# FFN blocks turned by transposing transfers of 16-bit halves instead of by TensorE

## The chip, the cores and the metric

The kernel runs on one core of a Trainium2 chip. Time is device microseconds of one execution of the whole program; the median of three runs is given. The engines are TensorE (PE), VectorE (DVE), ScalarE (ACT), GpSimd (POOL) and SyncE (SP); SP only issues transfers here, and POOL mostly. Each engine takes its instructions in order, and waits where one of them waits.

## The reference, cut to what matters

One layer of a streaming encoder on 512 tokens of width 1024, in float32:

```
x = x + 0.5 * swiglu(rms_norm(x, ffn1_norm), ffn1_w1, ffn1_w3, ffn1_w2)
h = rms_norm(x, mix_norm); p = h @ w_in               # RWKV-7, attention and gate columns
x = x + (gate_a * y_a + gate_b * y_b) @ w_out         # y_a from RWKV-7, y_b from attention
x = x + 0.5 * swiglu(rms_norm(x, ffn2_norm), ffn2_w1, ffn2_w3, ffn2_w2)
out = rms_norm(x, final_norm)

def swiglu(h, w1, w3, w2):
    return (silu(h @ w1) * (h @ w3)) @ w2             # w1, w3: 1024 x 2816, w2: 2816 x 1024
```

The change touches the two FFNs alone.

## The kernel before, in words

The products of float32 matrices are made of three TensorE matmuls each (`mm3`): both operands are split into a high part in a format that the array takes and the low rest; high by high, high by low, low by high. ACT casts the high part, DVE subtracts for the low one.

The hidden units of an FFN are 22 groups of 128. Two of them are computed one by one at the start; the other 20 are five blocks (0 to 4) of 512 units, class `Wide`. A block multiplies with the two-by-two scheme that needs seven products in place of eight: the tokens are two halves of 256, the contraction two halves of 512, and `w1` and `w3` give the other factors. Product n of block b is called the step (b, n), n from 0 to 6. One step is 24 matmuls of 128x512: two halves h of the weights, two halves i of the tokens' rows, two k, three of `mm3`. The weights of a step are sums of parts of `w1` and `w3` that transfers add up: plain loads on SP's queue (`plain`), adding ones on POOL's (`add`). `weight(m + 2, h)` splits the weights of the step after next in the middle of step m (h = 0) and at its end (h = 1), into a ring of four places; it also starts the next transfer into the buffer that it read.

The order of the steps is a list, `s.order`, m counting through it. Blocks 0 and 1 run interleaved at the start; from block 2 on the pattern repeats: (b, 0), two steps that finish block b-1, then (b, 1), (b, 2), (b, 6), (b, 5). What DVE, ACT and PE do stands in the program in the order in which they run (`written(True)`); the places of SP's and POOL's transfers among each other come from the scheduler.

Sums of the products stand in PSUM: X, Y and others, two banks each. `finish(m)` reads them after a step. After (b, 4) DVE adds into `u2` (the tile `u[0]`) and multiplies with `p`, after (b, 3) ACT takes the silu into `sa`, and DVE multiplies `u3` (`u[1]`) with it. `u[0]` and `u[1]` then hold the block's hidden values with tokens on the partitions: `u[half]` is 128 x 2 x 512, two groups i of 128 tokens. The second matrix, `w2` (class `Seven`), wants hidden units on the partitions, so each of the block's four groups f of 128 units is turned: `turn_all` makes 16 TensorE transposes of 128x128 a block into the banks Y (freed by then), and ACT copies four banks into their places in the tiles `rl` and `rh` (`hidden`). They run in the steps (b+1, 1) and (b+1, 2), in two sets of eight with an ACT copy pair each; for block 0 both sets run in (1, 2). Block 4, the last, is turned by `turn` in another place.

The tiles that the step of the change uses: `u` (`u_384`, `u_385` in FFN1), `p` (four tiles, two a block), `sa` (two), `rl`, `rh`. A transposing transfer is in the kernel before already: `tokens` (line 1083) splits a tile of 32-bit values into its low and high 16-bit halves by ACT (line 1086), turns them by a transposing transfer of SP (line 1087), and joins the halves on POOL (line 1089). It runs eight times, ahead of and at the start of FFN2.

Of the kernel before, what the change touches and what calls it, by code (L numbers as in the profile page):

```python
# [12 lines left out]
U16 = mybir.dt.uint16  # L13
# [6 lines left out]
P = 128  # L20
# [62 lines left out]
def kernel(  # L83
# [6 lines left out]
    nc = tc.nc  # L90
# [17 lines left out]
    dve, act, pe = [Queued(e, False) for e in (nc.vector, nc.scalar, nc.tensor)]  # L108
# [22 lines left out]
    ident = cp.tile([P, P], F32, name="ident")  # L131
# [368 lines left out]
    KH, TH, LO, HI = KF // 2, T // 2, slice(0, D // 2), slice(D // 2, D)  # L500

    BLOCKS, EARLY = (KF - 2) // 4, 2
# [147 lines left out]
    class Wide:  # L650


        def __init__(s, hp, kind, nrm, w1, w3, w2, quads, residual, C=None):
            def four(name):
                return [hp.tile([P, 2, T], F32, name=f"{name}{h}")[:] for h in range(2)]

            s.nrm, s.w, s.x, s.residual, s.later = nrm, (w1, w3), quads, residual, ()
            s.seven = sv = kind(hp, w2)
            s.A, s.B, s.C = [four("ca"), four("cd")], four("cb"), C or four("cc")
            s.extra = hp.tile([P, 2, T], F32R, name="extra")  # L660
            s.u = [hp.tile([P, 2, T], F32, name=f"u{i}")[:] for i in range(2)]
            q = [hp.tile([P, 2, 4, TH], F32R, name=f"q{i}") for i in range(3)]
            s.q = {n: (t[:, 0], t[:, 1]) for n, t in zip((1, 4, 3), q)}
            s.small = [hp.tile([P, NB], F32, name=f"sm{n}") for n in range(5)]
            s.end = BLOCKS - 1
            s.order = [(b, n) for n in (0, 6) for b in range(EARLY)]
            s.order += [(0, 1), (0, 2), (0, 4), (0, 5), (1, 1), (0, 3), (1, 2), (1, 4), (1, 5)]
            for b in range(EARLY, BLOCKS):
                s.order += [(b, 0), (b - 1, 3), (b - 1, 4)][:3 if b > EARLY else 2] + [(b, n) for n in (1, 2, 6, 5)]
            s.order += [(s.end, 4), (s.end, 3)]  # L670
            sv.parts = kind.PARTED
            e, o = [t[:].rearrange("p a t -> p (a t)").rearrange("p (b d) -> p b d", b=2) for t in quads]
            flat = [t.rearrange("p a t -> p (a t)") for t in (*s.C, *s.u)]
            sv.wide, sv.fg = s, flat[2]
            sv.O = [o[:, 0], o[:, 1], flat[0], flat[1]]
            sv.e = [t.rearrange("p (k t) -> p k t", t=TH) for t in (e[:, 0], e[:, 1], flat[3][:, 0:3 * TH])]
            a1, a0 = s.chain(s.end - 1), s.chain(s.end)
            sv.sum = [*a1, *s.B, a0[0], a0[1][:, 0:1]]
# [111 lines left out]
                cols = slice(half * TH, (half + 1) * TH)  # L790
                act.copy(s.seven.hidden(2 + 4 * s.end + f)[:, cols], s.turns[f][:, cols])

        def turn_all(s, b, fs):
            for f in fs:
                ps = s.Y[b % 2][f % 2]
                for i in range(4):
                    pe.transpose(ps[:, i * P:(i + 1) * P], s.u[i // 2][:, i % 2, f * P:(f + 1) * P], ident[:])
            for f in fs:
                act.copy(s.seven.hidden(2 + 4 * b + f), s.Y[b % 2][f % 2][:])

        def finish(s, m):
            b, n = s.order[m]
# [95 lines left out]
        def blocks(s, pa, pb, more):  # L898
            sv, end, nrm = s.seven, s.end, s.nrm
            raw = [[t[k][:, 0:TH] for k in range(KD)] for t in (nrm.hi, nrm.lo)]  # L900
            soon = {(0, 0): ((s.sums, 1),), (0, 6): ((s.low, 1),), (1, 6): ((s.low, 2),), (0, 1): ((s.low, 4),),
                    (0, 2): ((s.low, 5),), (0, 5): ((s.low, 3),)}
            todo = {(0, 0): ((s.gated, 0),),
                    (1, 0): ((s.cast, 1), (s.sums, 2)),
                    (0, 6): ((s.cast, 2), (s.sums, 4), (s.back, 0)),
                    (1, 6): ((s.cast, 4), (s.sums, 5), (s.hidden, 1, pa[:], pb[:])),
                    (0, 1): ((s.cast, 5), (s.gated, 1)),
                    (0, 2): ((s.cast, 3),),
                    (0, 5): ((s.cast, 0),),
                    (0, 3): ((s.low, 0), (s.cast, 6)),  # L910
                    (1, 2): ((s.low, 6), *[(s.plain, sv.O[i], s.residual[i]) for i in range(2)]),
                    (2, 5): ((sv.second, 0),), (3, 2): ((sv.two, 0),),
                    (end, 0): ((sv.operand, 0, 0),), (end, 2): ((sv.operand, 0, 1),), (end, 6): ((sv.one, 0),),
                    (end, 5): ((sv.second, 1), (sv.one, 1)), (end, 4): ((sv.two, 1),)}
            for at, steps in more.items():
                todo[at] = tuple(todo.get(at, ())) + steps
            for m, (b, n) in enumerate(s.order):
                apart = n == 4 and (b < EARLY or b == end)
                early = m < 2 * EARLY
                ps = s.X[b % 2] if n in (0, 2, 3, 5) or early else s.X[(b + 1) % 2] if n == 6 or apart else s.Y[b % 2]  # L920
                onto = n in (2, 3, 5) or (n == 6 and early) or (n == 4 and not apart)
                last = m + 2 >= len(s.order)
                if last:
                    sv.slots += s.ring[2 * m % 4:2 * m % 4 + 2]
                for h in range(2):
                    wh, wl = s.ring[(2 * m + h) % 4]
                    for i in range(2):
                        for k in range(2):
                            c = slice(i * P, (i + 1) * P)
                            if early:  # L930
                                qh, ql = [t[4 * (n > 0) + 2 * h + k][:, c] for t in raw]
                            else:
                                qh, ql = [t[:, 2 * h + k, c] for t in s.q[n]]
                            mm3(ps[i][:], qh, ql, wh[:, k], wl[:, k], not onto and h + k == 0, h + k == 2, onto)
                    if b > 1 and (n, h) == (2, 0):
                        s.turn_all(b - 1, (2, 3))
                    if (b, n) == (1, 2):
                        s.turn_all(0, ((0, 1), (2, 3))[h])
                    if h == 1:
                        if m == len(s.order) - 1:  # L940
                            s.turns = dict(zip((0, 2, 1, 3), s.Y[end % 2] + s.X[1 - end % 2]))
                            act.activation(s.sa[0], ps[0][:], AF.Silu)
                            act.activation(s.sa[1], ps[1][:], AF.Silu)
                            s.turn((0, 2), 0)
                            for i in range(2):
                                dve.tensor_tensor(s.u[1][:, i], s.u[1][:, i], s.sa[i], op=ALU.mult)
                            sv.operand(0, 2)
                        else:
                            s.finish(m)
                        if b > 1 and n == 1:  # L950
                            s.turn_all(b - 1, (0, 1))
                    if h == 1:
                        for f, *a in soon.get((b, n), ()):
                            f(*a)
                    if not last:
                        s.weight(m + 2, h)
                    elif len(sv.slots) == 2:
                        sv.weight(0, h)
                    elif h == 0:
                        sv.slots.insert(2, s.last)  # L960
                        sv.weight(0, 2)
                        sv.weight(0, 3)
                    else:
                        sv.weight(0, 4)
                s.gate(m)
                for f, *a in todo.get((b, n), ()):
                    f(*a)
            sv.slots.append(tuple(tmp("g5", (P, 1, T), F32R)[:] for _ in range(2)))
            sv.junk = [tmp(f"osq{i}")[:] for i in range(2)]
            sv.weight(0, 5)  # L970
            sv.run()
# [121 lines left out]
    with ExitStack() as mx:  # L1093
# [102 lines left out]
        for o, c0, mu in ((spare[2], DA, 4), (spare[3], 0, 0)):  # L1196
            ps = bank("pk", pf)
# [3 lines left out]
        for p in range(NP):  # L1201
            za.append((zslots[2 * p], zslots[2 * p + 1]))
            for i, (w_, x_, par0, o) in enumerate(((uw, lw, PAR_W0, zslots[2 * p]), (ux, lx, PAR_A0, zslots[2 * p + 1]))):
                ps = bank("pz", (pr, pf)[i])
# [181 lines left out]
        for t in range(C - 1):  # L1386
            n, m = t + 1, C - 1 - t
# [103 lines left out]
        at = b1.go(range(2))  # L1491
# [9 lines left out]
        at = b1.go(range(2, 5), a0.sum(at))  # L1501
# [3 lines left out]
        at = b1.go(range(5, 7), b0.sum(at))  # L1505
# [16 lines left out]
        at = ahead.go(range(7))  # L1522
# [254 lines left out]
        sees, turned, exps, copies, yb = [], ([], []), [], [], []  # L1777
# [176 lines left out]
        ycs, sqs, pgs, pus, parts = [None] * NP, [None] * NP, [None] * NP, [None] * NP, {}  # L1954
# [70 lines left out]
        ps = proj(0, fox_proj, ybs, fws[0])  # L2025
        for m in range(KD):
# [11 lines left out]
            if m + 1 < KD:  # L2038
                ps = proj(m + 1, fox_proj, ybs, fws[m + 1])
# [29 lines left out]
        for m in range(KD):  # L2069
            g = slot[m]  # L2070
            ps = proj(m, rwkv_proj, ya)
# [136 lines left out]
```

## Time and profile before

| | |
|---|---|
| median of 3 runs | 1082.62 us (1082.43 to 1082.85) |
| profiled execution | 1083.12 us, span 1081.3 us |
| busy: PE / DVE / ACT / POOL | 1072.1 / 829.7 / 677.4 / 223.9 us |
| granted TensorE clock | 0.999 |
| FFN1, steps of the blocks | from 33.3 us on |
| FFN2, first transposing load of its input | 712.4 us |
| bytes moved | 179.23 MB, mean 166 GB/s |

A row of a group or of the sequence reads: line, engine, operation, what is written <- what is read, shapes, how many; then busy time or start and length. `[0.30 <-PE P]` behind a row says how long the engine stood idle ahead of it and what ended that. Line 103 is that of the recording helper through which DVE, ACT and PE instructions pass, so many groups carry it. `SPq` and `POOLq` rows are transfers being issued; their time there is that of the issuing engine, not of the transfer.

### The profile page before, as it was taken

The numbers are of one execution on the slowest core, as the hardware profiler recorded it, in microseconds if no ns is written. First come the engines' busy times: TensorE is split into PE (matmuls) and PEld (weight loads), VectorE is DVE, ScalarE is ACT, GpSimd is POOL, SyncE is SP. The second block draws the span as 40 slices with busy tenths as digits, with TensorE's granted clock in tenths as the row PEclk, the third lists the DMA queues.
The fourth block names the chain that finished last, engine by engine and source line by source line (L and its number), as shares of the span: only waits on it lengthen the run. The fifth ranks groups of instructions, "written<-read, shape, count | busy, mean of one in ns | idle before, by whom it ended". The sixth has DMA issues, their size and how long they took to land.

```text
span 1081.3 us, 16859 instructions
## 1 busy us (share of the span) xinstructions
PE 1072.1 (99%) x6346; PEld 881.2 (81%) x6346; DVE 829.7 (77%) x1155; ACT 677.4 (63%) x1063; POOL 223.9 (21%) x275
## 2 busy tenths in 40 slices
PE   9999999999999999999999999999999999999997
PEld 7888888888887887888878887888888888888886
DVE  7998575789865698888777777866697666699874
ACT  6775556576555666445888876545576555576554
POOL 1221120134202302412000120125321212114210
PEclk9999999999999999999999999999999999999999
DMA  7989978769955443444312244677977979869972
GB/s 209 261 174 229 217 164 207 180 150 187 233 138 167 110 115 95 128 136 118 89 46 81 91 133 148 192 161 205 290 156 178 211 197 188 194 147 203 235 189 78
DMA packets 150543, 179.23 MB, mean 166 GB/s; under 512 B 20542, under 2 KB 86654, under 8 KB 150462
## 3 DMA queue, kind: packets, MB, share of 16 engines
q0 software_dynamic: 33392, 70.14, 33.8%
q1 hardware_dynamic: 116334, 106.58, 33.1%
q10 hardware_dynamic: 736, 1.45, 0.3%
q8 instruction: 50, 0.82, 0.3%
q14 instruction: 31, 0.25, 0.1%
HBM read 163.51 MB, written 12.52 MB: 163 GB/s over the span
## 4 chain that ended last, share of the span: by engine, by line
PE 96%; DVE 2%; ACT 1%; issue 1%; DMA 0%; ACTq 0%; DVEq 0%
PE P L103 40%; PE P L176 6%; PE P L175 6%; PE P L177 6%; PE pgt L103 5%; PE l L103 3%; PE spot L103 3%; PE pq L103 3%; PE ppj L103 2%; PE pk L177 2%; PE pk L175 2%; PE pk L176 2%; PE pw L176 1%; PE pw L177 1%; PE pw L175 1%; PE f L103 1%
## 5 line engine op out<-in xcount | busy, mean ns | idle before, releaser
L103 PE MATMUL P<-sraw,q 128*128 128x512 f32 x344 | 91.3, 389 | 0.0
L103 PEld LDWEIGHTS P<-sraw,q 128*128 128x128 f32 x344 | 64.6, 188 | 13.4
L103 PE MATMUL P<-swhi,q 128*128 128x512 f32 x224 | 71.4, 390 | 0.0
L103 PE MATMUL P<-sraw,wxh 128*128 128x512 f32 x200 | 68.4, 394 | 0.0
L167 ACT CAST whi<-raw 128x1024 fp32r<-128x1024 f32 (+2 forms) x42 | 40.4, 961 | 43.3 <-issue 14.2
L103 PE MATMUL P<-swhi,wxh 128*128 128x512 f32 x144 | 56.9, 395 | 0.0
L103 PE MATMUL P<-swhi,wxl 128*128 128x512 f32 x144 | 56.1, 390 | 0.0
L103 PE MATMUL P<-swlo,wxh 128*128 128x512 f32 x144 | 56.1, 389 | 0.0
L168 DVE TENSOR_TENSOR wlo<-raw,whi 128x1024 fp32r<-128x1024 f32 (+2 forms) x43 | 48.5, 1127 | 9.4 <-ACT whi L167 8.3
L693 POOL DMA_DIRECT2D cd<-in_ffn_w_dram x24 | 29.5, 1229 | 119.2 <-DVE swlo L103 38.3
L693 POOL DMA_DIRECT2D cb<-in_ffn_w_dram x20 | 24.1, 1207 | 144.7 <-DVE cd L103 80.0
L103 PE MATMUL P<-sraw,wxl 128*128 128x512 f32 x136 | 53.0, 390 | 0.0
L103 PEld LDWEIGHTS P<-swhi,q 128*128 128x128 f32 x224 | 42.1, 188 | 8.7
L103 PE MATMUL P<-swlo,q 128*128 128x512 f32 x112 | 43.6, 389 | 0.0
L103 ACT CAST sraw<-cd 128x1024 fp32r<-128x1024 f32 x30 | 31.5, 1050 | 19.0 <-PE P L103 11.5
L103 ACT COPY RD<-spot 32x128 f32<-32x128 f32 (+2 forms) x128 | 39.9, 311 | 5.3 <-PE spot L103 2.3
L103 PEld LDWEIGHTS P<-sraw,wxh 128*128 128x128 f32 x200 | 37.2, 188 | 7.3
L552 POOL DMA_DIRECT2D ca<-in_ffn_w_dram x16 | 19.3, 1205 | 95.8 <-DVE swlo L103 66.5
L103 DVE TENSOR_TENSOR u<-P,u 128x512 f32<-128x512 f32 x52 | 34.1, 684 | 5.8 <-ACT u L103 5.6
L103 DVE TENSOR_TENSOR swlo<-cc,swhi 128x1024 fp32r<-128x1024 f32 x20 | 24.5, 1225 | 18.2 <-ACT swhi L103 17.9
L177 PE MATMUL pk<-xh,wlo 128*128 128x512 f32 x96 | 37.5, 392 | 1.0 <-DVE wlo L168 1.0
L175 PE MATMUL pk<-xh,whi 128*128 128x512 f32 x96 | 38.0, 396 | 0.4 <-DVE u L1241 0.4
(626 smaller groups left out, 3434.4 us busy)
## 6 DMA issues: line engine op xcount, KB each, us to landing
raw<-in_w_in_dram SPq DMA_DIRECT2D x40, 512.0 KB
cc<-in_ffn_w_dram SPq DMA_DIRECT2D x36, 512.0 KB
cb<-in_ffn_w_dram POOLq DMA_DIRECT2D x36, 512.0 KB, 6.1
cb<-in_ffn_w_dram SPq DMA_DIRECT2D x32, 512.0 KB
cd<-in_ffn_w_dram POOLq DMA_DIRECT2D x32, 512.0 KB, 7.4
ca<-in_ffn_w_dram POOLq DMA_DIRECT2D x32, 512.0 KB, 7.3
ca<-in_ffn_w_dram SPq DMA_DIRECT2D x20, 512.0 KB
cd<-in_ffn_w_dram SPq DMA_DIRECT2D x18, 512.0 KB
```

Of the source, the lines that this page charges most:

```text
L103: q.last = do(*a, **kw)
L167: (hi_eng or act).copy(hi[:], raw[:])
L168: (eng or dve).tensor_tensor(lo[:], raw[:], hi[:].bitcast(F32), op=ALU.subtract)
L175: pe.matmul(ps, whi, xhi, start=first, stop=False, skip_group_check=onto)
L176: pe.matmul(ps, whi, xlo, start=False, stop=False, skip_group_check=onto)
L177: return pe.matmul(ps, wlo, xhi, start=False, stop=last, skip_group_check=onto)
L552: nc.gpsimd.dma_start(s.sum[g], src, accum_op=ALU.add)
L693: nc.gpsimd.dma_start(to, s.block(b, n, h), accum_op=ALU.add)
```

## The change

For blocks 0 to 3 of both FFNs the 16 TensorE transposes and four ACT copies of `turn_all` are gone. In their place, at the end of the step that finishes a half (n = 4 finishes `u[0]`, half 0; n = 3 finishes `u[1]`, half 1), `apart` copies each 128 x 512 group of `u[half]` by ACT into 16-bit halves, low ones first, then high ones, 1024 of them; it puts them into `p[b]` (half 0) or `sa` (half 1), which are free then. SP turns each by one transposing transfer of eight 128x128 tiles back into `u[half]`. Three steps later, after the weight split in the middle of the step, `joined` interleaves the halves again by four ACT copies into the places in `rl` and `rh`. Block 4 is turned as before. For blocks 2 and 3 the two finishing steps swap: (b, 4) comes ahead of (b, 3).

```
-                s.order += [(b, 0), (b - 1, 3), (b - 1, 4)][:3 if b > EARLY else 2] + [(b, n) for n in (1, 2, 6, 5)]
+                s.order += [(b, 0)] + [(b - 1, 4)] * (b > EARLY) + [(b - 1, 3)] + [(b, n) for n in (1, 2, 6, 5)]
...
-        def turn_all(s, b, fs):
-            for f in fs:
-                ps = s.Y[b % 2][f % 2]
-                for i in range(4):
-                    pe.transpose(ps[:, i * P:(i + 1) * P], s.u[i // 2][:, i % 2, f * P:(f + 1) * P], ident[:])
-            for f in fs:
-                act.copy(s.seven.hidden(2 + 4 * b + f), s.Y[b % 2][f % 2][:])
+        def apart(s, b, half):
+            for i in range(2):
+                parts = (s.sa if half else s.p[b])[i].bitcast(U16)
+                act.copy(parts.rearrange("p (s c) -> p s c", s=2), s.u[half][:, i].bitcast(U16).rearrange("p (c s) -> p s c", s=2))
+                nc.sync.dma_start(s.u[half][:, i].bitcast(U16).rearrange("p (a t) -> p a t", t=P), parts, transpose=True)
+
+        def joined(s, b, half):
+            turned = s.u[half].rearrange("p i t -> p (i t)").bitcast(U16).rearrange("p (i s f t) -> p f i t s", i=2, s=2, t=P)
+            for f in range(4):
+                to = s.seven.hidden(2 + 4 * b + f)[:, half * TH:(half + 1) * TH].bitcast(U16)
+                act.copy(to.rearrange("p (i t s) -> p i t s", i=2, s=2), turned[:, f])
...
+            joins = []
...
-                    if b > 1 and (n, h) == (2, 0):
-                        s.turn_all(b - 1, (2, 3))
-                    if (b, n) == (1, 2):
-                        s.turn_all(0, ((0, 1), (2, 3))[h])
...
-                        if b > 1 and n == 1:
-                            s.turn_all(b - 1, (0, 1))
...
+                    for at, half, b_ in joins:
+                        if (m, h) == (at, 0):
+                            s.joined(b_, half)
+                if n in (3, 4) and b < end:
+                    s.apart(b, int(n == 3))
+                    joins.append((m + 3, int(n == 3), b))
```

What this does to the order of instructions is shown at two places of FFN1's block 3, whose finishing steps are (3, 4) and (3, 3). The first place is TensorE where the block was turned, around the steps (4, 1) and (4, 2); `P_501` and `P_502` are the banks Y, `u_384` and `u_385` the tiles `u[0]` and `u[1]`.

```order
 L103 MATMUL P_500<-swlo,q_386 128x512
 L103 MATMUL P_500<-swhi,q_386 128x512
-L103 MATMUL P_501<-ident,u_384 128x128 x2
-L103 MATMUL P_501<-ident,u_385 128x128 x2
-L103 MATMUL P_502<-ident,u_384 128x128 x2
-L103 MATMUL P_502<-ident,u_385 128x128 x2
 L103 MATMUL P_495<-sraw,wxh_507 128x512 x2
 L103 MATMUL P_495<-sraw,wxl_508 128x512
```

The eight transposes between the steps are gone and nothing stands in their place; eight more are gone from the middle of (4, 2).

The same place on ScalarE, from the weight split of step (3, 4)'s end to the joining of half 0 (`swhi`, `sraw` are high parts of weights):

```order
 L103 CAST swhi<-cd_379 128x1024
+L103 CAST swhi<-cd_380 128x1024
+L103 COPY p_503<-u_384 128x1024
+L103 COPY p_504<-u_384 128x1024
+L103 CAST sraw<-cd_379 128x1024
 L103 ACTIVATE sa_455<-P_497 128x512
 L103 ACTIVATE sa_456<-P_498 128x512
-L103 CAST swhi<-cd_380 128x1024
-L103 CAST sraw<-cd_379 128x1024
 L103 CAST sraw<-cd_380 128x1024
+L103 COPY sa_455<-u_385 128x1024
+L103 COPY sa_456<-u_385 128x1024
```

The splitting copies of half 0 now stand ahead of the next weights' cast and of the silus into `sa`, and those of half 1 behind them. The joining copies follow later in the same program:

```order
 L103 CAST sraw<-cb_381 128x1024
+L103 COPY rl_372<-u_384 128x512
+L103 COPY rh_375<-u_384 128x512
+L103 COPY rl_373<-u_384 128x512
+L103 COPY rh_376<-u_384 128x512
 L103 COPY u_384<-P_495 128x512
```

They read the turned tile `u_384` where the old copies read the banks, and stand ahead of the copies that write the next block's values into `u_384`. The second place is SP's queue around the same steps (`cc`, `ca` are weight buffers):

```order
 L555 DMA ca_377<-in_ffn_w_dram 128x2x512
 L555 DMA ca_378<-in_ffn_w_dram 128x2x512
-L690 DMA cc_363<-in_ffn_w_dram 128x2x512
-L690 DMA cc_364<-in_ffn_w_dram 128x2x512
+L797 DMA_TRANSPOSE u_384<-p_503 128x8x128
+L797 DMA_TRANSPOSE u_384<-p_504 128x8x128
+L797 DMA_TRANSPOSE u_385<-sa_455 128x8x128
+L797 DMA_TRANSPOSE u_385<-sa_456 128x8x128
```

Four transposing transfers now stand in SP's queue between the loads of the weights; behind them follow the loads of `cc`.

## The prediction

> **What bounds the kernel now.** I read the page first (busy times, the chain that ended last), then TensorE's waits, then the transposes themselves.
>
> ```profile
> PE 1072.1 (99%) x6346; PEld 881.2 (81%) x6346; DVE 829.7 (77%) x1155; ACT 677.4 (63%) x1063; POOL 223.9 (21%) x275
> PE 96%; DVE 2%; ACT 1%; issue 1%; DMA 0%; ACTq 0%; DVEq 0%
> PE warm L312 <- DVE onesr L137: 1.1, 1, 1.1
> PE pk L177 <- DVE wlo L168: 1.0, 2, 0.7
> PE pk L175 <- DVE u L1241: 0.4, 1, 0.4
> ```
>
> TensorE (PE) is busy 99% of the span and is 96% of the chain. The three last rows are all that it waited for: 2.5 us, and none of it in an FFN. So in the FFNs an instruction taken from PE shortens the kernel by the time that it holds the array, and any other engine costs nothing until it makes PE wait.
>
> **What the removed transposes cost.** First the group, then the sequence around one set of eight.
>
> ```profile
> L103 PE MATMUL P<-ident,u x160: 270/272/277, 90.3 to 975.1; 128*128 128x128 f32 x160
> 90.06 0.39 PE L103 MATMUL P<-sraw,wxl 128*128 128x512 f32 x1
> 90.30 1.03 PE L103 MATMUL P<-ident,u 128*128 128x128 f32 x8
> 91.08 0.48 PE L103 MATMUL P<-sraw,wxh 128*128 128x512 f32 x1
> 91.40 0.39 PE L103 MATMUL P<-extra,wxh 128*128 128x512 f32 x1
> 91.63 0.40 PE L103 MATMUL P<-sraw,wxl 128*128 128x512 f32 x1
> ```
>
> There are 160; the change removes the 16 of each of four blocks in both FFNs, 128 in 16 sets of eight, and keeps 32 (the last blocks). The 272 ns of one are no price, since they overlap. The price is what a set adds to the spacing of starts. Matmuls with nothing between start 0.227 us apart (the two `sa` rows further down are six matmuls and 1.36 us apart). From 90.06 to 91.40 there are two such steps, 0.45 us, but 1.34 us pass: a set costs **0.89 us** (0.78 for the eight, 0.11 for the changes in and out). 16 x 0.89 = **14.2 us** off PE. I take this whole.
>
> **What is added, and what hides it.** One step (24 matmuls) is 24 x 0.227 = 5.44 us; a block has seven. The rows below are from FFN1, where block 3 finishes; a step ends where ACT can begin on its second bank, here 191.2.
>
> ```profile
> 189.84 0.60 ACT L103 ACTIVATE sa<-P 128x512 f32<-128x512 f32 x1 [0.30 <-PE P L103]
> 191.20 0.60 ACT L103 ACTIVATE sa<-P 128x512 f32<-128x512 f32 x1 [0.76 <-PE P L103]
> 191.69 1.04 ACT L103 CAST swhi<-cd 128x1024 fp32r<-128x1024 f32 x1
> 202.52 0.59 ACT L103 COPY rl<-P 128x512 f32<-128x512 f32 x1 [2.07 <-PE P L103]
> 203.00 0.59 ACT L103 COPY rh<-P 128x512 f32<-128x512 f32 x1
> 190.85 1.23 DVE L103 TENSOR_TENSOR cd<-cd,cb 128x1024 f32<-128x1024 f32 x1
> 192.00 1.29 DVE L103 TENSOR_TENSOR u<-u,sa 128x512 f32<-128x512 f32 x2
> 196.73 1.28 DVE L103 TENSOR_TENSOR u<-P,u 128x512 f32<-128x512 f32 x2
> 197.93 1.28 DVE L103 TENSOR_TENSOR u<-u,p 128x512 f32<-128x512 f32 x2
> 160.00:200.00 40.00, 40.00 (x186) 33.32 (x185) 27.62 (x29) 22.99 (x30) 7.26 (x6) 1.00 0.82 185
> 880.00:920.00 40.00, 40.00 (x186) 33.29 (x186) 27.67 (x29) 21.93 (x28) 7.26 (x6) 1.00 0.83 185
> ```
>
> (The last two are 40 us stretches: length, busy PE, PEld, DVE, ACT, POOL, the clock, the DMA share, GB/s.) The trace has the same operations once: FFN2's input is split into 16-bit halves by ACT and turned by transposes on SP's queue, and POOL waits for them.
>
> ```profile
> 732.67 1.13 ACT L1086 COPY G<-xS 128x512 uint16<-128x512 uint16 x2
> 723.69 1.24 SPq L1087 DMA_TRANSPOSE G<-G  x1
> 734.45 1.72 SPq L1087 DMA_TRANSPOSE G<-G  x1
> 757.62 8.51 SPq L1087 DMA_TRANSPOSE rh<-rh  x1
> 766.24 4.48 SPq L1087 DMA_TRANSPOSE rl<-rl  x1
> 729.21 1.44 POOL L1089 COPY G<-G 128x512 uint16<-128x512 uint16 x2 [2.45 <-DMA G<-G]
> 739.03 1.88 POOL L1089 COPY G<-G 128x512 uint16<-128x512 uint16 x2 [2.12 <-DMA G<-G]
> 775.05 2.84 POOL L1089 COPY rl<-rl 128x512 uint16<-128x512 uint16 x2 [0.24 <-DMA rl<-rl]
> ```
>
> *ScalarE.* Per half two splitting copies of 1024 halfwords and four joining ones of 512. Two 512-wide copies with a step of two take 1.13 us here, so 2 x 1.1 + 4 x 0.6 = 4.6 us; a block has two halves, 9.2 us, and loses four copies from PSUM (0.59 each): +6.8 us a block, 54 us in all. ACT is busy 22 to 23 of 40 us there and would be at some 29 of 38. It stays hidden as long as the casts that PE needs are not late.
>
> *The path of one half.* Take 191.2, in the times of before, as the end of step (3,4), which now comes first. DVE is free at 192.0, subtracts the two tiles until 193.2 (the `u` pairs start 1.20 apart) and has the first product some 0.7 later, 193.9. ACT copies until 195.0 and 196.1, and SP issues the two transfers then. The joining copies stand behind ACT's cast in the middle of the third step after: 191.2 + 2.5 x 5.44 = 204.8, plus 0.3 to the cast and 1.05 for it: 206.2. So the second transfer has **10.1 us**, the first 11.2. Alone one took 4.58 us (734.45 to 739.03) to 5.52 (723.69 to 729.21) from issue to POOL's start, of which 1.24 and 1.72 hold SP, so two in a row should have landed 1.7 + 5.5 = 7.2 us after 195.0, at 202.2: 4.0 us early. If they are late, ACT waits, and the weight casts, `u`'s copies and DVE stand behind it. The first that PE needs are the two copies of `u`, which free the bank that step (4,5) adds to at 191.2 + 4 x 5.44 = 213.0; with 1.1 us for them and 2.1 for four joins (starts 0.48 apart) the joins may begin at 209.8. Only a lateness beyond 3.6 us reaches PE. The other half runs 5.2 to 5.4 us later with the same room: issued at 200.3 and 201.3, wanted at 211.6, free until 215.2. Cost taken: **0**; bounds 0 and what the rivals give.
>
> *SP and POOL queues.* SP's loads behind the transposes in its queue (the next block's fourth product) are issued once DVE has freed their buffer, about 203.6 (their cast in the middle of step (4,1), behind ACT's copies), when SP, done with the last transfer at 201.3 + 1.7, is free; the cast of what they bring comes in the middle of the fifth step after 191.2, at 215.7, 12 us later, where loads on POOL's queue land in 6.1 to 7.4 us:
>
> ```profile
> cb<-in_ffn_w_dram POOLq DMA_DIRECT2D x36, 512.0 KB, 6.1
> cd<-in_ffn_w_dram POOLq DMA_DIRECT2D x32, 512.0 KB, 7.4
> ```
>
> *DMA engines.* How much room a transfer takes, by the stretches of the existing ones:
>
> ```profile
> 706.00:712.00 6.00, 6.00 (x28) 4.76 (x27) 4.46 (x7) 3.23 (x5) 0.00 (x0) 1.00 0.51 139
> 717.90:723.00 5.10, 5.10 (x24) 4.21 (x23) 2.63 (x5) 2.61 (x4) 3.43 (x4) 1.00 0.88 206
> 990.00:1010.00 20.00, 20.00 (x90) 16.57 (x89) 20.00 (x21) 11.71 (x13) 10.29 (x9) 1.00 1.10 199
> ```
>
> One transfer and one 256 KB store lift the share from 0.51 to 0.88 of 5.1 us, so a transfer takes at most 1.9 us of all engines; four in a 38.1 us block add 0.20 to 0.82: 1.02. In the third row the share is 1.10 and PE is still busy for all of 20.00 us. Reordering (b,4) before (b,3) leaves one step (5.44 us) instead of two between the subtraction that reads bank Y and the next product added to it; that subtraction ends some 3 us after its step. No cost.
>
> **The sum.** The profiled execution took 1083.12 us (span 1081.3), 0.5 above the median 1082.62. 1083.12 - 14.2 = 1068.9 for such an execution, so 1068.4 against the median. I say **1068.5 us**.
>
> **Rivals.**
>
> *1. Transfers in series, and PE waits (slower).* For it: under the burst of loads that opens FFN2, the pair issued at 757.62 landed at 775.05, 17.4 us, and SP itself was held for 8.5 and 4.5 us. With 8.7 us each in series the first half lands at 195.0 + 17.4 = 212.4, 2.6 us after 209.8, and the second 17.4 later at 229.8, against 215.2 + 2.6: 12.0 more. 14.6 us a block, eight blocks, less 14.2: +103 us, **1185**. It decides from 1.8 us a block on (14.2 / 8): four in series from 195.0 that end after 215.2 + 1.8 = 217.0, that is more than 5.5 us each, which is the longest that one took alone. Against it: those 5.5 hold the latency, which overlaps if SP can issue the next, and a block's stretch has no burst of ten loads. The Trainium skill speaks for this rival: "VectorE: DVE Perf Modes" (The three transpose paths; Rules for kernel authors) gives 1309 ns for a 128x128 16-bit tile by DMA against 390 ns on TensorE and advises TensorE where PSUM will do. Estimate by that figure: eight tiles a transfer, 10.5 us, 41.9 a block, more than the block lasts. The rows (4.58 to 5.52 us for eight) stand nearer to the forecast. 0.11.
>
> *2. A little late everywhere.* With six us each in places, or ACT pushed by its 6.8 us, PE waits 0.5 to 1.5 us a block: 1 x 8 = 8 us, **1076.5**. For it: 4.0 us of margin is little. Against: 3.6 us more before PE feels it. 0.13.
>
> *3. Only the first block pays.* Where FFN1 leaves its early steps, ACT already stands 4.26 us behind DVE:
>
> ```profile
> 74.05 1.19 ACT L103 COPY P<-rh 128x512 f32<-128x512 f32 x2 [4.26 <-DVE u L103]
> 82.12 1.22 DVE L103 TENSOR_TENSOR swlo<-cd,swhi 128x1024 fp32r<-128x1024 f32 x1
> 33.28 214.59 PE P L103 x987
> ```
>
> The two splitting copies (2.1 us) come right behind and hold up the casts. That `swlo` ends at 83.34 and PE wants it in the middle of the tenth step, 33.28 + 9.5 x 5.44 = 85.0; if all of the 2.1 us reached it, it would be late, and the casts after it too. A slip of 1 to 2 us in each FFN costs 3 us: **1071.5**. 0.08.
>
> *4. Nothing gained*: the slots are filled by waits elsewhere, **1082.6**. PE waits for nothing in the FFNs, so little speaks for it. 0.03.
>
> **How the numbers follow.** The forecast has 0.65. The range 1067.0 to 1077.0 holds it with rival 3 and most of 2 (0.65 + 0.08 + 0.09, 0.82); below 1067 there is nothing more to remove. Faster by over 0.2% (2.2 us, about what this kernel's timing tells from nothing): forecast, rival 3 and most of 2, 0.83; within it 0.06 (rival 4 and the bad end of 2); slower 0.11 (rival 1).
>
> **What would show it.** Right: 128 fewer `P<-ident,u`, PE busy about 1058, no wait of PE on `u`, `sraw` or `swhi` in the FFNs, ACT near 732 busy, and the first joining copy of each half ended by PE or nothing, not by a transfer. Wrong: rows in which ACT's joining copies wait for `u<-p` or `u<-sa` for more than 3.6 us and PE then for casts; SP held far over 2 us per transpose; casts that wait for `cc` loads.

## The result, and the profile after

The changed kernel takes **1095.18 us** (median of four executions, 1092.15 to 1098.97) against 1082.53 beside it: ratio **1.0118** (95%: 1.0087 to 1.015). It is slower by 12.7 us; 1068.5 was predicted, with 1067 to 1077 as the range. The profiled execution took 1095.48 us, span 1093.7. An execution over 1.5% above the fastest of its kernel is left out of medians, ranges and ratios; that is one each in two runs below (1088.7 and 1089.7 us).

The page of the kernel after, its busy times and its chain, then the two longest lines of TensorE's waits, both new (engine and line that waited, who ended it: us in total, times, longest):

```profile
PE 1064.5 (97%) x6218; PEld 868.4 (79%) x6218; DVE 832.0 (76%) x1155; ACT 721.9 (66%) x1127; POOL 223.2 (20%) x275
PE 75%; DMA 8%; DVE 7%; issue 5%; ACT 3%; POOL 0%; SPq 0%; DVEq 0%; ACTq 0%; POOLq 0%
PE P L103 <- DVE p L103: 10.2, 2, 5.6
PE P L103 <- DVE u L103: 4.8, 6, 1.9
```

The 128 transposes are gone (6346 to 6218 matmuls), but PE is busy only 7.6 us less instead of 14.2, and it is idle for 1093.7 - 1064.5 = 29.2 us, where it was idle for 1081.3 - 1072.1 = 9.2. Transfers and DVE have taken a part of the chain that was PE's. What ACT waits for, in the same kernel:

```profile
ACT rl L103 <- DMA u<-sa: 19.2, 4, 6.6
ACT swhi L103 <- DMA cc<-in_ffn_w_dram: 18.5, 2, 9.7
ACT swhi L103 <- DMA cd<-in_ffn_w_dram: 6.5, 2, 5.5
```

The joining copies of half 1 (`u<-sa`) waited four times; those of half 0 (`u<-p`) do not appear. The casts of `cc` waited twice, once in each FFN, and that is the wait that reached PE. The sequence of FFN1's last block shows how, engine by engine:

```profile
190.97 1.20 POOL L693 DMA_DIRECT2D cb<-in_ffn_w_dram  x1 [9.09 <-DVE cd L103]
193.57 3.65 SPq L797 DMA_TRANSPOSE u<-p  x2
195.76 1.20 POOL L693 DMA_DIRECT2D cb<-in_ffn_w_dram  x1 [3.59 <-DVE cd L103]
197.00 1.20 POOL L693 DMA_DIRECT2D cd<-in_ffn_w_dram  x1
198.41 8.20 SPq L797 DMA_TRANSPOSE u<-sa  x2
199.34 1.20 POOL L693 DMA_DIRECT2D cd<-in_ffn_w_dram  x1 [1.13 <-DVE extra L103]
206.71 2.12 SPq L690 DMA_DIRECT2D cc<-in_ffn_w_dram  x2
207.70 1.07 ACT L103 CAST q<-rl 128x1024 fp32r<-128x1024 f32 x1
217.54 1.04 ACT L103 CAST swhi<-cc 128x1024 fp32r<-128x1024 f32 x1 [8.77 <-DMA cc<-in_ffn_w_dram]
218.62 1.23 DVE L103 TENSOR_TENSOR swlo<-cc,swhi 128x1024 fp32r<-128x1024 f32 x1 [8.42 <-ACT swhi L103]
219.76 1.28 DVE L103 TENSOR_TENSOR p<-P,p 128x512 f32<-128x512 f32 x2
220.59 0.76 PE L103 MATMUL P<-swhi,q 128*128 128x512 f32 x1 [4.64 <-DVE p L103]
```

Read it from the top. Four adding loads of POOL (`cb`, `cd`) stand around half 1's two transposing transfers, which hold SP for 8.20 us; half 0's, with one adding load ahead of them, hold it for 3.65. The load of `cc` behind them is issued at 206.71 and lands at 217.5, 10.8 us later. ACT has been free since 208.77. DVE's subtraction for these weights waits for ACT's cast, and behind it, in DVE's order, stands the sum into `p` that frees the bank PE needs. PE does not wait for a transpose or for `cc`; it waits for `p`, three instructions down the line.

What the DMA engines did meanwhile, as windows (length, busy PE, PEld, DVE, ACT, POOL, clock, DMA share, GB/s), first the kernel before, then the one after:

```profile
160.00:175.00 15.00, 15.00 (x76) 12.60 (x75) 8.12 (x8) 7.82 (x12) 1.41 (x2) 1.00 0.91 218
```

```profile
160.00:175.00 15.00, 15.00 (x68) 12.41 (x67) 8.00 (x8) 7.50 (x10) 1.20 (x1) 1.00 1.33 122
160.00:200.00 40.00, 39.07 (x171) 31.66 (x170) 26.96 (x28) 28.09 (x37) 6.68 (x6) 1.00 1.13 207
```

Between 160 and 175 us block 2's half 1 is turned (its pair holds SP from 157.71 for 8.62 us): the engines are at a share of 1.33 and move 122 GB/s; before, 0.91 and 218. They are full and move little.

### The profile page after: what moved, and what is told of

It is laid out like the page before. It is cut to its first block, busy times and chain, and to the rows that moved or that the text cites. A ratio compares the mean times of both kernels' runs of the same rounds, so it can differ in the third digit from the quotient of the medians.

```text
span 1093.7 us, 16755 instructions
## 1 busy us (share of the span) xinstructions
PE 1064.5 (97%) x6218; PEld 868.4 (79%) x6218; DVE 832.0 (76%) x1155; ACT 721.9 (66%) x1127; POOL 223.2 (20%) x275
## 2 busy tenths in 40 slices
DMA packets 184336, 187.62 MB, mean 172 GB/s; under 512 B 54334, under 2 KB 120446, under 8 KB 184254
## 3 DMA queue, kind: packets, MB, share of 16 engines
q0 software_dynamic: 33392, 70.14, 35.0%
## 4 chain that ended last, share of the span: by engine, by line
PE 75%; DMA 8%; DVE 7%; issue 5%; ACT 3%; POOL 0%; SPq 0%; DVEq 0%; ACTq 0%; POOLq 0%
PE P L103 22%; PE P L177 5%; PE P L175 5%; PE P L176 5%; PE pgt L103 5%; PE l L103 3%; PE spot L103 3%; DMA u<-sa 3%; PE pq L103 3%; DMA cc<-in_ffn_w_dram 2%; PE ppj L103 2%; PE pk L175 2%; PE pk L177 2%; PE pk L176 2%; PE pw L176 1%
## 5 line engine op out<-in xcount | busy, mean ns | idle before, releaser
L103 PE MATMUL P<-swhi,q 128*128 128x512 f32 x224 | 74.1, 402 | 11.0 <-DVE p L103 10.2
L167 ACT CAST whi<-raw 128x1024 fp32r<-128x1024 f32 (+2 forms) x42 | 40.3, 960 | 43.7 <-issue 14.2
L176 PE MATMUL pk<-xl,whi 128*128 128x512 f32 x96 | 37.5, 391 | 0.0
```

Source lines behind the costliest of these rows:

```text
L103: q.last = do(*a, **kw)
L167: (hi_eng or act).copy(hi[:], raw[:])
L176: pe.matmul(ps, whi, xlo, start=False, stop=False, skip_group_check=onto)
```

## The experiments

The theory after the traces: *the transposing transfers share the DMA engines badly with the adding loads of the same steps; half 1's and the `cc` load behind them are late, and in the last block that reaches PE.* Rivals: the added ACT copies (they are on the way of every cast); SP's queue alone; the bytes, not the turning; lateness that gathers over the blocks.

**The transfers taken out.** The transfer's line is deleted, so the blocks are not turned; the joining copies read the same tile in another pattern.

```
-                nc.sync.dma_start(s.u[half][:, i].bitcast(U16).rearrange("p (a t) -> p a t", t=P), parts, transpose=True)
```

> The changed kernel without its transposing transfers; ScalarE's splitting and joining copies stay, and the joining ones read the tile unturned (so the hidden units of four blocks reach the second matrix unturned: part of the computation is left out). Theory A (the transfers, by being late and by holding SP's queue, cost all that was lost): 1068.5 us, 1067 to 1071, and no wait of TensorE above 1 us in the FFNs. Rival B (ScalarE's extra copies, 45 us by the page of the change, push the casts late): 1080 us or more.

1072.34 us, ratio 0.9906 (0.9892 to 0.9921). All ACT copies, the order and the waits among engines are there, and the time is 23 us below the change. So ACT's added work is hidden, and the loss lies in the transfers.

**The same bytes, not turned.**

```
-                nc.sync.dma_start(s.u[half][:, i].bitcast(U16).rearrange("p (a t) -> p a t", t=P), parts, transpose=True)
+                nc.sync.dma_start(s.u[half][:, i].bitcast(U16), parts)
```

> The changed kernel with each transposing transfer replaced by a plain one of the same 256 KB between the same tiles on the same queue (the values stay unturned). Theory A1 (turning is what makes a transfer slow: 184,336 packets against 150,543, about 1,000 of under 512 B for each): 1069 to 1073 us. Rival A2 (any further 8 MB on SP's queue at these places does it): 1088 us or more.

1072.49 us, ratio 0.9907 (0.9892 to 0.9921): like no transfer at all. The place of half 1's transfers in SP's queue, in this kernel:

```profile
194.60 1.42 SPq L797 DMA_DIRECT2D u<-sa  x2
197.76 2.01 SPq L690 DMA_DIRECT2D cc<-in_ffn_w_dram  x2
```

1.42 us of SP against 8.20, same queue, same 2 x 256 KB. It is the turning that costs, not the bytes nor one more transfer in the queue. A turned transfer also goes in more packets (184,336 in all on the page, against 155,152 here); no run separates that from the turning.

**Block 3 back on TensorE** (blocks 0 to 2 by transfers).

```
-                if n in (3, 4) and b < end:
+                if n in (3, 4) and b < end - 1:
+        # turn_all of before, for b - 1 == 3 alone, in the steps (4, 1) and (4, 2)
```

> Blocks 0 to 2 of each FFN turned by transfers, block 3 by TensorE as before. Theory C (of 13.4 us lost in FFN1 some 11 are lost in the last block, where the load of cc for (4,4) was issued at 206.7, behind the transposes, and landed at 217.5): 12 sets gone are 10.7 us, about 2.4 us of small stalls stay in each FFN, so 1082.5 - 10.7 + 4.8 = 1076.6, 1075 to 1079. Rival D (every block's transfers cost about the same): 1082.5 + 12.6 x 6/8 = 1092.

1077.2 us (1074.8 to 1079.66), ratio **0.9943** (0.9927 to 0.996): faster than before, and within the 1075 to 1079 expected. Three of four blocks by transfers gain 5.2 us where 12 sets are worth 10.7, so 5.5 us are lost there too; the fourth block turned the gain into the loss.

**Block 3 alone by transfers**, the counterpart.

```
-                if n in (3, 4) and b < end:
+                if n in (3, 4) and b == end - 1:
+        # turn_all of before for blocks 0 to 2, in the places of before
```

> Only block 3 is turned by transfers, blocks 0 to 2 by TensorE: the counterpart of the run with blocks 0 to 2. If the loss lies in the last block, where the load of cc for step (4,4) has only two steps, and does not need the transfers of the blocks before: PE waits 4 to 6 us for p once in each FFN and each FFN loses 8 to 11 us there, less two sets of eight transposes (1.8): 1094 to 1102 us. If lateness gathers over the blocks (DMA engines that never catch up): block 4 is hardly late and the kernel takes 1080 to 1086.

1097.76 us (1097.14 to 1097.91), ratio 1.0139 (1.0126 to 1.0152). TensorE's first wait and ACT's first wait for loads of this kernel:

```profile
PE P L103 <- DVE p L103: 8.4, 2, 5.1
ACT swhi L103 <- DMA cc<-in_ffn_w_dram: 16.7, 2, 9.3
```

The net loss is there whole, with nothing turned by transfers in the blocks before: 15.2 us slower although four sets (3.6 us) are gone, so block 3's transfers cost 18.8 us. Lateness that gathers over the blocks falls.

**The `cc` load on another queue.** For the last block it goes to POOL's queue, past SP's transposes.

```
+                if end:
+                    nc.gpsimd.dma_start(here, s.block(b, 4, h))
-                if b != 1:
+                elif b != 1:
                     s.plain(here, s.block(b, 4, h))
```

> The changed kernel with one load moved: the weights of step (4,4), 2 x 512 KB into cc, are issued on GpSimd's queue instead of SP's, where they stood behind the transposes. Theory C1 (SP's queue, held 8.2 us by the second pair, makes that load late): it is issued at about 202 instead of 206.7 and lands by 211, TensorE's wait of 4.6 us and the slow clock behind it go: about 8 us less in each FFN, 1079 us, 1076 to 1084. Rival C2 (the DMA engines are full, share 1.3 there, so the order in the queue does not matter): 1092 to 1098.

1100.3 us (1098.35 to 1103.62), ratio 1.0167 (1.0145 to 1.0189): no better, and above both ranges expected. Its POOL, SP and ACT:

```profile
204.75 0.76 POOL L715 DMA_DIRECT2D cc<-in_ffn_w_dram  x1 [1.30 <-DVE swlo L103]
201.32 12.02 SPq L799 DMA_TRANSPOSE u<-sa  x2
220.54 1.04 ACT L103 CAST swhi<-cc 128x1024 fp32r<-128x1024 f32 x1 [8.90 <-DMA cc<-in_ffn_w_dram]
```

The load is issued as soon as its buffer is free, 204.75, and still lands at 220.5, 15.8 us later. Time saved in the queue is lost at the DMA engines: SP's queue is where the wait stood, not why.

**The transfers by themselves.** A kernel that computes nothing: groups of transfers, each group begun when the last one has landed; a copy by DVE (`seen<-dst`) or ACT (`seen<-wt`) of two elements shows each landing. Its transposing and its adding transfer:

```
nc.sync.dma_start(dst[i][:].rearrange("p (a t) -> p a t", t=P), src[i][:], transpose=True)
nc.gpsimd.dma_start(wt[i][:], weights(i), accum_op=ALU.add)
```

> Transfers by themselves, with no other work: one transpose of 128 x 1024 halfwords, twice; four in a row, twice; four adding loads of 512 KB alone; four transposes with four adding loads, twice; six plain loads of 512 KB alone; four transposes with six plain loads; four plain copies of the same bytes alone; four plain copies with four adding loads. The layer is not computed. Theory T1 (transposes are slow whatever runs beside them, and follow one another in series): one lands 4.5 to 5.5 us after issue, four take 16 us or more also alone, and plain loads or adding loads change that by less than a third. Theory T2 (they are slowed by the adding loads): four alone land within 10 us, 12 us or more beside adding loads, within 11 beside plain loads. Theory T3 (any load slows them): four alone within 10 us, 12 us or more beside either kind. In all three the plain copies of the same bytes land within 8 us alone and 10 beside adding loads.

DVE's sequence, for four transposes alone (begun behind the `src` row), with four adding loads (the second such group), and with six plain loads:

```profile
18.41 0.10 DVE L24 MEMSET src<- 128x1 uint32 x4
21.86 0.17 DVE L24 COPY seen<-dst 128x2 uint16<-128x2 uint16 x1 [3.35 <-DMA dst<-src]
...
25.76 0.17 DVE L24 COPY seen<-dst 128x2 uint16<-128x2 uint16 x1 [1.02 <-DMA dst<-src]
...
71.07 0.36 DVE L24 MEMSET wt<- 128x2 f32 x4
74.21 0.17 DVE L24 COPY seen<-dst 128x2 uint16<-128x2 uint16 x1 [2.77 <-DMA dst<-src]
86.73 0.17 DVE L24 COPY seen<-dst 128x2 uint16<-128x2 uint16 x1 [12.35 <-DMA dst<-src]
94.67 0.17 DVE L24 COPY seen<-dst 128x2 uint16<-128x2 uint16 x1 [7.77 <-DMA dst<-src]
95.56 0.17 DVE L24 COPY seen<-dst 128x2 uint16<-128x2 uint16 x1 [0.73 <-DMA dst<-src]
...
107.06 0.56 DVE L24 MEMSET wt<- 128x2 f32 x6
112.14 0.17 DVE L24 COPY seen<-dst 128x2 uint16<-128x2 uint16 x1 [4.52 <-DMA dst<-src]
...
123.81 0.17 DVE L24 COPY seen<-dst 128x2 uint16<-128x2 uint16 x1 [0.62 <-DMA dst<-src]
```

| group | last transpose, copy or (where alone) load landed after | spacing |
|---|---|---|
| 4 transposes of 256 KB alone | 7.4 us | 1.2 to 1.4 us |
| 4 plain copies of 256 KB alone | 4.5 us | 0.66 us |
| 4 transposes with 4 adding loads of 512 KB | 22.8 and 24.6 us | |
| 4 transposes with 6 plain loads of 512 KB | 16.9 us | |
| 4 plain copies with 4 adding loads | 8.7 us | |
| 4 adding loads alone | 14.1 us | 2.5 us per 512 KB |
| 6 plain loads alone | 10.7 us | 1.35 us per 512 KB |

A transpose alone is quick: 3.4 us to landing, 1.2 to 1.4 us behind another (the four above are 7.4 us together), so T1 falls. Beside four adding loads the second one lands 13 to 16 us after the group began, where a plain copy in its place took 3.3 (129.0 to 132.33); T2's first half holds. Its second half does not: plain loads slow transposes too, 16.9 us, which is T3's number. The plain loads there are 3 MB in a row, though, the adding ones 2 MB. In both mixes the group takes about the sum of its parts: 7.4 + 10.7 = 18.1 us for the plain loads, 7.4 + 14.1 = 21.5 for the adding ones. The kernel itself has to say which loads matter there.

**The adding loads made plain, in the changed kernel.** The sums of the weights are left out; bytes, places and queue are the same.

```
-            nc.gpsimd.dma_start(to, s.block(b, n, h), accum_op=ALU.add)
+            nc.gpsimd.dma_start(to, s.block(b, n, h))
```

> The changed kernel with the adding loads of the FFN blocks replaced by plain loads of the same bytes into the same places on the same queue, so the sums of the weights are left out and the result is another one. T2 (adding loads are what slows the transposes): every half in time, 1071 to 1075 us, no wait of PE for p. T3 or T1 (any traffic, or the transposes themselves): joins of half 1 still wait 4 to 7 us, PE still waits some 5 us for p in each FFN, 1088 to 1096 us.

**1071.54 us** (1071.19 to 1072.08), ratio 0.9898 (0.9884 to 0.9912), with all 32 transposing transfers. Its page, SP's rows and ACT's at the place shown above:

```profile
PE 1058.0 (99%) x6218; PEld 866.6 (81%) x6218; DVE 830.1 (78%) x1155; ACT 724.7 (68%) x1127; POOL 196.0 (18%) x275
188.67 2.62 SPq L797 DMA_TRANSPOSE u<-p  x2
193.52 3.13 SPq L797 DMA_TRANSPOSE u<-sa  x2
196.74 1.73 SPq L690 DMA_DIRECT2D cc<-in_ffn_w_dram  x2
204.76 1.05 ACT L103 CAST swhi<-cc 128x1024 fp32r<-128x1024 f32 x1
```

Half 1 holds SP for 3.13 us, `cc` is issued at once, and neither its cast nor the joins wait. The window from 160 to 175 us, at 1.33 and 122 GB/s in the change, has 0.87 and 235 here. With the run of plain copies this settles which transfers do it: the transposes with plain loads cost little (1071.5 us), the adding loads with plain copies cost little (1072.5), the two together cost over 20 us. What stays open is why: an adding load also holds the engines almost twice as long (2.5 us to 1.35) and goes in more packets (33,392 on POOL's queue against 25,712 here, for the same 70.14 MB), and no run separates that from a conflict of the two kinds.

**The order alone**: the kernel before with only the swap of (b, 3) and (b, 4).

> The kernel before with only the swap of the finishing steps, (b, 4) ahead of (b, 3); the blocks are turned by TensorE. If the swap costs nothing, as the prediction took it: 1082.4 us (1081.8 to 1083). If the shorter distance between the subtraction and the next product in the same bank is felt, or the turns wait for u: 1084 or more. Its middle stage should last the 522.6 us of before; if the swap were what lengthens it, 524.

1082.63 us, ratio 1.0 (0.9991 to 1.0009). The swap costs nothing, as the prediction had it.

**Versions that gain.** First, block 3's second half by TensorE in one set of eight, and half 1 of blocks 1 and 2 joined a step later:

```
+                        if b == end and n == 1:
+                            s.turn_all(b - 1)          # half 1 alone, eight transposes
-                    joins.append((m + 3, int(n == 3), b))
+                    joins.append((m + 3 + int(n == 3 and b > 0), int(n == 3), b))
```

> Block 3's second half is turned by TensorE (8 transposes at the end of step (4,1)); the halves of blocks 0 to 2 and block 3's first half stay with the transfers, and the second halves of blocks 1 and 2 are joined one step later (at the fourth step after, still ahead of the copy that writes the tile again). If only the second halves come late and only block 4's cc load suffers, as the trace of the change says: the 1072.4 us of the run without transfers plus two sets of eight transposes (2 x 0.89), 1074.2 us (1073.5 to 1076), below the kernel before and below the run with three blocks. If the first half of block 3 is enough to delay the cc load: 1078 to 1086.

Median 1077.7 us, but executions from 1071.3 to 1084.4; ratio 0.9952 (0.9931 to 0.9972). The median lies between the two ranges expected. Without the last block's trouble the same lateness comes out elsewhere, as this row of ACT in block 3 shows:

```profile
183.18 1.04 ACT L103 CAST swhi<-cc 128x1024 fp32r<-128x1024 f32 x1 [8.98 <-DMA cc<-in_ffn_w_dram]
```

Then block 3 wholly by TensorE, as above, with the same line for the later join:

> Block 3 wholly turned by TensorE, as in the run with three blocks, and the second halves of blocks 1 and 2 joined one step later. If the lateness of second halves is what kept that run (1077.2 us) from the sum: 1072.4 + 4 sets x 0.89 = 1076.0 us (1075.5 to 1077), with a narrow spread. If ACT's waits at the joins cost nothing there: the same 1077.2 as that run.

Median 1077.9 us, 1072.5 to 1086.3, ratio 0.9958 (0.9933 to 0.9983). Not the 1076.0 expected, and a wider spread than the run with three blocks. A later join alone moves ACT's wait from the join to the next cast, as the row above shows for the run before this one.

Then the transfers themselves moved, with four blocks turned as in the change: half 1 of blocks 1 to 3 is split and transferred one step later, behind the adding loads, and joined one step later.

```
-                if n in (3, 4) and b < end:
+                if b < end and (n == 4 or (b, n) == (0, 3)):
                     s.apart(b, int(n == 3))
                     joins.append((m + 3, int(n == 3), b))
+                elif n == 3 and b < end:
+                    joins.append((m + 4, 1, b))
+                for at, half, b_ in joins:
+                    if b_ and half and at == m + 3:
+                        s.apart(b_, 1)
```

> All four blocks by transfers, but the second half of blocks 1 to 3 is split and transferred one step later (after step (b+1,1)) and joined one step later too. In the trace of the change the four adding loads that ACT's and DVE's splits of that place release (148.9 to 157.3 in the runs without a wait) are then landed, and the first cc load stands ahead of these transfers in SP's queue. If the collision of the four transfers with the four adding loads is the cause: 1072 to 1076 us, PE waiting less than 2 us for p and u. If four transfers a block are too many wherever they stand: 1084 to 1096, with cc or the joins late.

1079.93 us (1074.85 to 1085.81), ratio 0.9978 (0.9959 to 0.9998). With the same 32 transposing transfers 15 us of the change's time are back; its first PE wait is `u`, and ACT's waits are those of other places:

```profile
PE P L103 <- DVE u L103: 3.7, 6, 2.1
ACT swhi L103 <- DMA cd<-in_ffn_w_dram: 10.0, 3, 5.9
ACT swhi L103 <- DMA cc<-in_ffn_w_dram: 3.8, 2, 2.6
```

Of 18.5 us for `cc` 3.8 are left, and the joins wait 1.6 us in place of 19.2. What remains is `cd`: in FFN1 its two adding loads go out at 100.08 and 103.62, block 1's first half at 102.69, and the second cast waits for its load until 118.14. SP is held there for 6.40 us by the pair of half 0. That place was not moved. The time lies between the two ranges expected.

The last run has both, block 3's half 1 by TensorE and the later transfers of blocks 1 and 2:

> The second halves of blocks 1 and 2 split and transferred one step later, as in the run before; block 3's second half turned by TensorE, its first half and block 0 by transfers as in the change. Removed from PE: 14 of the 16 sets. If collisions were settled by that: 1072.4 + 2 x 0.89 = 1074.2 us (1073.5 to 1076.5) with a spread of 3 us or less, the fastest correct kernel here. If two transfers near adding loads still make cd or cc late now and then, as the run with the later step showed (its executions lay from 1074.9 to 1085.8): a median of 1076.5 to 1080 and a spread of 8 us or more.

**1076.59 us** (1074.88 to 1081.12), ratio **0.9944** (0.9931 to 0.9958). With the run of three blocks (0.9943) it is the best here that computes the layer: 5.8 us below the kernel before (1082.36 beside it). The median lies in the range expected if loads are still late now and then; the spread, 6.2 us, lies between the 3 and the 8 us expected. PE's first wait in it is 5.3 us for casts, and ACT's is 16.0 us for `cd`, the loads that remained late in the run before.

## Why the prediction was wrong

**What was right.** ACT's copies are hidden: with all of them and no transfers the time is 1072.3. ACT was busy 721.9 us, near the 732 forecast. The swap is free. Half 0 was never late in the change. And 14.2 us off PE was right: where transfers are not late PE is busy for 1058.0, the 1058 predicted. The forecast itself was still 3 us too low for such a kernel (1071.5, not 1068.5). Of that 2 us come back in the middle stage, in which nothing was changed: DVE waits for `Ls`, a round trip of POOL's through memory. First the run without transfers, then the kernel before, each with DVE's row, and for the former what it did to PE:

```profile
459.20 0.19 DVE L1393 TENSOR_TENSOR prod<-TT,Ls 128x31 f32<-128x31 f32 x1 [5.43 <-DMA Ls<-Ld]
PE pv L176 <- DVE wlo L168: 1.1, 1, 1.1
```

```profile
464.38 0.19 DVE L1389 TENSOR_TENSOR prod<-TT,Ls 128x31 f32<-128x31 f32 x1 [3.44 <-DMA Ls<-Ld]
```

Between the FFNs this run needs 524.7 us where before has 522.6. The `Ls` wait gives 1.1 of the 2.1; the rest was not followed. The other 1 us and a little more are waits of PE for `u`: in the run with the adding loads made plain, matmul against matmul with the kernel before, some 0.7 us are lost in each FFN where block 4 is turned. The price of a set was right: by the same comparison each set that is gone brings 0.88 to 0.89 us.

**The step that failed first: "DMA engines".** It sized a transfer at 1.9 us "of all engines", added four of them to a share of 0.82, got 1.02, and called that harmless since PE stood a share of 1.10 elsewhere. The size was too high for a transfer alone, which takes 1.2 to 1.4 us. The addition was wrong: the stretch from 160 to 200 has 1.13, and a share says how full the engines are, not how long the next transfer stands behind the others. Beside four adding loads the same four transfers take 22.8 to 24.6 us instead of 7.4. The stretch that the size was read from (717.9 to 723.0) holds a transpose beside a store. The trace before did show transposes held up, the pair at 757.62 with 8.51 and 4.48 us of SP, but this term left it out. That pair stands behind ten plain loads, and plain loads are enough: in the run with the adding loads made plain it is still held.

```profile
751.88 7.44 SPq L1092 DMA_TRANSPOSE rh<-rh  x1
759.42 3.43 SPq L1092 DMA_TRANSPOSE rl<-rl  x1
```

So what a transfer costs depends on how much is in flight beside it, and adding loads are not the only kind that can hold it up.

**Then "The path of one half".** "The other half runs 5.2 to 5.4 us later with the same room" copied half 0's path onto half 1's, and the cost was taken as 0. Their neighbours differ: three of the four adding loads are issued within 195.76 to 199.34, around half 1's transfers. SP was held 3.65 us for the one pair and 8.20 for the other. Half 1 had to come within 3.6 us of its time; ACT waited 6.6 us for it at worst, from the time that its joins came up.

**Then "SP and POOL queues"**, the term that cost most. It gave the `cc` load 12 us, to "the middle of the fifth step after 191.2", 215.7. That is the distance of a block in the repeating order. The last block has no next block's (b+1, 0) in between: its order ends (4, 6), (4, 5), (4, 4), so the cast stands in the middle of (4, 6), the fourth step: 191.2 + 3.5 x 5.44 = 210.2, and the room is 210.2 - 203.6 = 6.6 us for a load that lands in 6.1 to 7.4. The run with the adding loads made plain agrees: cast at 204.76, 8.0 us after the issue at 196.74. With no margin, both of the failures above went through to PE. Against that run, at the same step, half 0's transfers of the change start 4.9 us later (193.57 to 188.67), but `cc` 10.0 (206.71 to 196.74): 5.1 us are SP's hold. It then needed 10.8 us to land.

**The sum of the loss.** Against the run with the adding loads made plain, the span is 24.2 us longer: PE is idle 29.2 - 11.5 = 17.7 us more, and busy 6.5 more for the same 6218 matmuls. A part of that second number is the clock: right after the wait that ends at 220.59 matmuls start 0.43 us apart in place of 0.23, and the stretch's granted clock is 0.96:

```profile
221.15 0.63 PE L103 MATMUL P<-swlo,q 128*128 128x512 f32 x1
221.58 1.06 PE L103 MATMUL P<-swhi,q 128*128 128x512 f32 x2
200.00:240.00 40.00, 33.21 (x143) 26.70 (x142) 25.91 (x27) 26.51 (x37) 3.69 (x4) 0.96 0.87 162
```

So a wait of 4.6 us there cost more than its length. Matmul against matmul in the two traces, the slow starts add 1.5 us behind each of the two waits for `p`; most of the other 3.6 lies in the waits themselves, whose first part the page counts as busy. By the same comparison 18.5 of the 24.2 us fall into the last blocks of the two FFNs (the waits for `p` with the slow starts 13.5, those for `u` ahead of block 4's turn 5.0) and 5.3 into the blocks before. That fits the 18.8 and 5.5 us of the runs with block 3 alone and with the other three.

**The rivals.** Rival 1 (transfers late, PE waits, slower; 0.11) is what happened, in kind. Its price, 103 us, was for every half of every block; most of the real one is in the last block of each FFN. It was put aside with "a block's stretch has no burst of ten loads": four adding loads are burst enough. The price from which it decides, 1.8 us a block, was passed: the loss of 24.2 us in eight blocks is 3.0 a block, against 11.0 us that the kernel gains where no transfer is late (1082.53 to 1071.54). Rivals 2 and 3 are in it as small terms, the 5.3 us of the blocks before the last. The page of the Trainium skill that spoke for rival 1 ("VectorE: DVE Perf Modes", The three transpose paths) gives 1309 ns for one 128x128 tile by DMA. No run here sends a single tile; eight in one transfer landed 3.4 us after the issue, and 1.2 to 1.4 us behind another. The same page's advice (Rules for kernel authors), TensorE where PSUM will do, holds here for the last block and not for the three before, whose transfers gain 5.2 us.

## What to carry to other kernels

Cost a transfer by what runs beside it in the same few microseconds, kind by kind, and not by its share of a long stretch: here 1.2 to 1.4 us behind another transpose, and up to 12 beside adding loads. Check each load's room in the first and the last turn of a loop separately; the repeating order says nothing about them. When an idle engine's work is moved to the DMA engines, look at which load is queued behind it and has the least room, since that is where PE will feel it, under the name of some other tile.

## What the runs showed of the hardware

- A transposing transfer of 256 KB (eight 128x128 tiles of 16 bits) lands 3.4 us after issue, and one follows another at 1.2 to 1.4 us: half the rate of a plain copy of the same bytes (0.66 us).
- Adding loads of 512 KB from memory, issued by POOL, land 2.5 us apart; plain ones, issued by ACT, 1.35.
- Transposes beside adding loads: 22.8 and 24.6 us for four of each, as much as or more than one after the other (7.4 + 14.1 = 21.5), while four plain copies beside the same loads were through in 8.7, and all of that group in 16.3. Beside six plain loads of 512 KB four transposes took 16.9 us (7.4 + 10.7 = 18.1 one after the other). SP was held for 18.37 us by the issue of four:

```profile
47.73 18.37 SPq L24 DMA_TRANSPOSE dst<-src  x4
```

- Executions of most kernels in which these meet differ more than others do: 1071.3 to 1084.4 us for one program, where the kernel before stays within 0.2%. Block 3 alone by transfers is an exception, with 1097.14 to 1097.91 us.
